# Moving the S5 parameters to GpSimd and the S5 factors to VectorE, and scaling the banded attention's weights without GpSimd

## The chip, the cores and the metric

The kernel runs on one core of a Trainium2 chip. The metric is the device time of one execution in microseconds (us). The core's engines work in parallel, each through its own queue of instructions in a fixed order, and wait for each other on semaphores: TensorE (PE in the profile; PEld is its weight load), VectorE (DVE), ScalarE (ACT), GpSimd (POOL) and SyncE (SP), which starts most of the DMA transfers. A measurement of this kernel tells about 0.3% from no change.

## The reference, cut to what matters

Two residual layers over 1024 tokens of width 1024. Only the first is touched by the change. Its input projection gives q, k, v and a gate for a banded attention with sinks, and u and a gate for an S5 state-space mixer:

```python
def swa_sink_attention(q, k, v, sinks, rel_bias):     # 8 blocks of 128 queries, 8 heads of 64, 2 kv heads
    ...                                               # each block sees its own and the previous 128 keys
    logits = jnp.where(mask[None, :, None, None], logits + bias, NEG_INF)
    p = jax.nn.softmax(jnp.concatenate([logits, sink], axis=-1), axis=-1)[..., :-1]
    out = jnp.einsum('bnhgqk,bnkhd->bnqhgd', p.astype(v.dtype), v_band)

def s5_mixer(u, log_dt, a_re, a_im, b_re, b_im, c_re, c_im, d_skip, glu_w, glu_b):
    dt = jnp.exp(log_dt)[:, None]                     # 32 groups of 64 states
    mag = jnp.exp(a_re * dt)
    ang = a_im * dt
    ab_re, ab_im = mag * jnp.cos(ang), mag * jnp.sin(ang)
    f_re = ((ab_re - 1) * a_re + ab_im * a_im) / (a_re * a_re + a_im * a_im)
    ...
    bb_re = f_re[..., None] * b_re - f_im[..., None] * b_im
    ...                                               # x_t = ab x_(t-1) + bb u_t, y_t = Re(c x_t) + d u_t
    h = jax.nn.gelu(y) @ glu_w + glu_b
    return h[..., :W] * jax.nn.sigmoid(h[..., W:])

def even_layer(hn, ...):
    q, k, v, gate_a, u, gate_b = split_cols(hn @ w_in, EVEN_SPLITS)
    ...                                               # rms norm of q and k by head
    return jnp.concatenate([att * silu(gate_a), ssm * silu(gate_b)], axis=-1) @ w_out
```

The second layer, a sparse attention with an indexer, follows.

## The kernel before

**Weights.** Every projection runs in three TensorE products, high half by high half, high by low and low by high. The weights come as a stream of chunks of 256 columns (8 pieces of 128 x 256): chunk 0 is u's first half, 1 is k and v, 2 is u's second half, 3 and 4 q, 5 and 6 the attention's gate, 7 and 8 the S5 gate, 9 and 10 the GLU, 11 to 18 the first output projection; the second layer's follow. `load_w` (L139) lets ScalarE round a chunk to its high half `whi` (L153) and another engine subtract to the low half `wlo` (L154). That engine is VectorE for the chunks of `LO_ON_V` (L126), in four instructions of 128x512, and otherwise GpSimd, in one of 128x2048 (save for chunks 21, 31 and 32). Such pieces are issued with priority when the stream runs ahead.

**The first 44 us** load x, split it and form u's first half. `mean_square` (L201) then gives 1 / rms of the 1024 tokens: VectorE forms the mean (L209, L210), GpSimd a power of 128x8 (L211), VectorE spreads it on a diagonal (L365), TensorE broadcasts it (L368) and ScalarE copies it to `rb` (L369). All of u's and the gates' results are multiplied by `rb` on VectorE.

**S5 parameters** (L438 to L539) are written next: some 120 VectorE instructions of 128x16, each with a small input from the one ahead. From the state matrix `aa` and the step `dt` they give an exponential (`exp_of`), sine and cosine (ScalarE), the input factors `fre`, `fim`, the powers `pw` of the transition by squaring, the unit rotations `ue` (seven, each squared from the one before and brought back to length one by `unit`), the table `T16` (products of `T` by `ue`, L523 to L528) and `Bb` (L534 to L539).

**Projections of k, v and u** (`u_chunk`, kv) come between. `norm_heads` scales by head: ScalarE squares and sums, GpSimd forms the factor `nr` in two small instructions (L199, L200), ScalarE scales, and for k GpSimd multiplies by the gains (L393).

**S5 quarters.** `s5_quarter` (L589) runs four times. VectorE forms the factors `Q` and `Tb` with `cmul` (L603 to L610 for the code that both engines share); GpSimd forms `W` with the same helper, in 20 instructions per quarter, since its buffer `tmpg` holds 256 elements. TensorE transposes Q into QT and multiplies QT by U (L674). VectorE rotates, scans (L687) and rotates back into X (L690 to L698); TensorE multiplies W by X (L707). While this runs, TensorE works on the remaining projections: the order of every engine's queue was set by a scheduler when the kernel was built, with priorities, so that the k, v, u, q and gate matmuls lie between the quarters' own.

**Banded attention** (215 us and on; after a stretch of gate projection alone, from 252 to 372 us). It runs in 16 units, of a block and a kv head with 4 query heads each. `swa_scores` (L759): TensorE makes scores (L767, L768), VectorE adds the bias and takes the row maximum (L769), ScalarE the exponentials of four heads of 128x256 (L774), VectorE the reciprocal of the sum, and then the weights are scaled: by VectorE in four instructions for kv head 0 (L781), by GpSimd in one of 128x1024 for kv head 1 (L778). `swa_out`: TensorE transposes the weights (L790), ScalarE or VectorE evicts them (L795, L793), and TensorE multiplies by v (L796). Between these lie 384 matmuls of gate projection (L232 to L234) and 36 of the GLU. The GLU, the output projection and the second layer (500 to 1077 us) follow.

## Time and profile before

| | us |
|---|---|
| median of 3 runs | 1075.03 (1072.58 to 1075.17) |
| the profiled execution | 1078.34 |
| its span in the trace | 1076.6 |
| TensorE matmul busy in it | 1012.1 |
| VectorE busy | 770.3 |
| ScalarE busy | 607.1 |
| GpSimd busy | 469.0 |

The granted TensorE clock is 0.983 of full speed on average. The profile gives busy time of each engine, and the views of the trace give each instruction's start and duration and, for idle time, what the engine waited for. A matmul's duration in the trace includes its way through the array: several overlap, so that the time from start to start, not the duration, is what one costs.

### The profile page before, as it was taken

To read this page: it belongs to the slowest core of one execution; us is meant where nothing else is said; L and a number is where in the kernel's file an instruction comes from. 1 tells how busy PE (TensorE), PEld (TensorE's weight loads), DVE (VectorE), ACT (ScalarE), POOL (GpSimd) and SP (SyncE) were. 2 spreads that over 40 slices of the span, in tenths; PEclk is the share of its full clock that TensorE was granted. 3 is DMA by queue.
4 is the path that set the end of the run, shared out by engine and by line. 5 is a ranking of instruction groups with operands and counts; after the bars stand their busy time and mean duration, and the time that the engine had idled before them with its cause. 6 is when DMAs were issued, how large, how long until landed. Compare 5 with 4: busy or idle time off the path is not lost.

```text
span 1076.6 us, 19055 instructions
## 1 busy us (share of the span) xinstructions
PE 1012.1 (94%) x6536; PEld 888.5 (83%) x6536; DVE 770.3 (72%) x1742; ACT 607.1 (56%) x1609; POOL 469.0 (44%) x647
## 2 busy tenths in 40 slices
PE   6898788999999899999999989999999879999998
PEld 4787788999877478887889989999887659898898
DVE  6999889635677675455469678889877997777742
ACT  6453344324545443444466789879976776565620
POOL 2267677332211212223031577867653947555000
PEclk9999899999999899999999999999999999999999
DMA  7282533594343324652011223022325745665333
GB/s 264 79 265 81 149 103 104 151 269 134 96 140 118 103 103 142 210 196 108 1 40 63 67 74 104 16 80 84 98 89 176 246 130 163 200 190 172 115 104 113
DMA packets 103697, 138.33 MB, mean 128 GB/s; under 512 B 9352, under 2 KB 79880, under 8 KB 98736
## 3 DMA queue, kind: packets, MB, share of 16 engines
q1 hardware_dynamic: 103600, 137.12, 39.9%
q8 instruction: 51, 0.84, 0.3%
q14 instruction: 46, 0.38, 0.1%
HBM read 102.31 MB, written 36.21 MB: 129 GB/s over the span
## 4 chain that ended last, share of the span: by engine, by line
PE 68%; DVE 16%; ACT 5%; DMA 4%; POOL 3%; issue 3%; SPq 1%; ACTq 0%; POOLq 0%; DVEq 0%
PE mm L234 7%; PE mm L232 7%; PE mm L233 7%; PE mm L218 4%; PE mm L219 4%; PE mm L220 4%; PE mm L1546 3%; PE mm L1547 3%; PE mm L1545 3%; PE tr L1396 2%; PE psx L796 2%; DVE tmp L687 1%; PE mm L1411 1%; PE mm L1412 1%; PE pq L1370 1%
## 5 line engine op out<-in xcount | busy, mean ns | idle before, releaser
L154 POOL TENSOR_TENSOR wlo<-wraw,whi 128x512 fp32r<-128x512 f32 (+1 forms) x50 | 101.1, 2047 | 111.6 <-ACT whi L153 106.1
L153 ACT CAST whi<-wraw 128x512 fp32r<-128x512 f32 (+2 forms) x122 | 84.3, 748 | 70.6 <-DMA wraw<-in_wo_dram 28.0
L219 PE MATMUL mm<-wlo,h1T_hi 128*128 128x256 f32 x384 | 109.5, 286 | 0.0
L1369 POOL TENSOR_TENSOR bt<-bt,mk 128x384 f32<-128x384 f32 (+3 forms) x80 | 83.8, 1066 | 59.0 <-DMA bt<-g_d 41.0
L218 PE MATMUL mm<-whi,h1T_hi 128*128 128x256 f32 x384 | 109.0, 286 | 0.2 <-DVE gst L976 0.2
L220 PE MATMUL mm<-whi,h1T_lo 128*128 128x256 f32 x384 | 108.9, 285 | 0.0
L1216 DVE TENSOR_SCALAR_CACHE_REDUCE vjunk<-sc,vt 128x512 bf16<-128x512 uint16 (+5 forms) x90 | 91.0, 1012 | 2.7
L233 PE MATMUL mm<-hT_lo,whi 128*128 128x256 f32 (+1 forms) x288 | 86.4, 300 | 0.0
L234 PE MATMUL mm<-hT_hi,wlo 128*128 128x256 f32 (+1 forms) x288 | 86.1, 299 | 0.0
L232 PE MATMUL mm<-hT_hi,whi 128*128 128x256 f32 (+1 forms) x288 | 86.0, 299 | 0.0
L1252 ACT ACTIVATE sjunk<-sc,st 128x384 bf16<-128x384 uint16 (+5 forms) x90 | 77.7, 864 | 6.8 <-POOL st L1256 4.7
L1545 PE MATMUL mm<-aT_hi,whi 128*128 128x256 f32 x256 | 73.0, 285 | 1.2 <-ACT aT_hi L1519 1.2
L218 PEld LDWEIGHTS mm<-whi,h1T_hi 128*128 128x128 f32 x384 | 72.3, 189 | 1.0 <-PE psi L1060 0.6
L1546 PE MATMUL mm<-aT_lo,whi 128*128 128x256 f32 x256 | 72.2, 282 | 0.7 <-DVE aT_lo L1520 0.7
L219 PEld LDWEIGHTS mm<-wlo,h1T_hi 128*128 128x128 f32 x384 | 72.4, 188 | 0.4
L220 PEld LDWEIGHTS mm<-whi,h1T_lo 128*128 128x128 f32 x384 | 72.2, 189 | 0.4
L1547 PE MATMUL mm<-aT_hi,wlo 128*128 128x256 f32 x256 | 72.1, 282 | 0.0
L391 ACT ACTIVATE st<-mm,nr 128x64 f32<-128x64 f32 (+1 forms) x160 | 45.5, 357 | 45.0 <-POOL nr L200 44.6
L154 DVE TENSOR_TENSOR wlo<-wraw,whi 128x512 fp32r<-128x512 f32 (+1 forms) x72 | 50.2, 737 | 25.3 <-ACT whi L153 22.7
L1067 DVE SCALAR_TENSOR_TENSOR sc<-relu,wi,sc 128x384 f32<-128x384 f32 (+3 forms) x70 | 49.4, 707 | 20.6 <-ACT relu L1062 16.9
L1380 ACT ACTIVATE s<-s,mn 128x384 f32<-128x384 f32 (+7 forms) x56 | 45.9, 820 | 26.9 <-DVE mn L1374 26.8
L1400 DVE TENSOR_TENSOR pT_lo<-tr,pT_hi 128x512 fp32r<-128x512 f32 x72 | 49.1, 685 | 15.7 <-ACT pT_hi L1399 15.6
(396 smaller groups left out, 3483.3 us busy)
## 6 DMA issues: line engine op xcount, KB each, us to landing
...
```

What stands on the lines that cost most here:

```text
L153: S.copy(hi[p_], raw[p_])
L154: eng.tensor_sub(lo[p_], raw[p_], rd(hi[p_]))
L218: T.matmul(ps, a, hi[:, k, c0:c1], start=(k == 0), stop=False)
L219: T.matmul(ps, a, lo[:, k, c0:c1], start=False, stop=False)
L220: T.matmul(ps, b, hi[:, k, c0:c1], start=False, stop=(k == 7))
L232: T.matmul(o, a, hT[0][:, k, ts], start=(k == 0), stop=False)
L233: T.matmul(o, a, hT[1][:, k, ts], start=False, stop=False)
L234: T.matmul(o, b, hT[0][:, k, ts], start=False, stop=(k == 7))
L1216: V.tensor_scalar(junk[:, :128 * (b + 1)], data(b), self.thr(j), None, op0=OP.is_ge, op1=OP.add, accum_out=self.cnt[:, it, j:j + 1])
L1545: T.matmul(ps, a, aT[0][:, k, toks], start=(k == 0), stop=False)
L1546: T.matmul(ps, a, aT[1][:, k, toks], start=False, stop=False)
L1547: T.matmul(ps, b, aT[0][:, k, toks], start=False, stop=(k == 7))
```

## The change

Four things change, all in the first layer.

1. **The S5 parameters go to GpSimd.** [...] 34 of them (the exponential of the step, the angle and its reduction) stand ahead of the power for 1 / rms; 115 behind it (the exponential for `mag`, the powers, the squarings and `unit`s of `ue`). An ordering (`issue_after`) holds the sine, the cosine and all that is written up to `Bb` behind the power, the diagonal and rb's copy. The factors `fre`, `fim`, the table `T16` and `Bb` stay on VectorE.
2. **W goes to VectorE**, in 16 instructions per quarter, since the helper's buffer for VectorE holds 512 elements.
3. **Low halves.** Chunks 9 to 12 (the GLU's two and the first two of the output projection) go to VectorE. Those that stay on GpSimd come in four instructions of 128x512.
4. **Scaling of the banded weights.** In every unit two heads are scaled by VectorE and two by ScalarE; GpSimd's instruction goes.

```diff
-    LO_ON_V = (0, 1, 2) + tuple(range(13, 21)) + (29, 30) + tuple(range(33, 39))
+    LO_ON_V = (0, 1, 2) + tuple(range(9, 21)) + (29, 30) + tuple(range(33, 39))
...
-        return (hi, lo), [piece, WSTEP if i in LO_ON_V or i in (21, 31, 32) else 8, 0]
+        return (hi, lo), [piece, WSTEP, 0]
...
-        G.tensor_tensor(r, r, neghalf[:, :n], op=OP.pow)
+        last_rms[0] = G.tensor_tensor(r, r, neghalf[:, :n], op=OP.pow).ins
...
-    def exp_of(sp, o, xin, n):
+    def exp_of(E, stt, sp, o, xin, n):
...
-        V.tensor_scalar(a, xin, 88.0, -87.0, op0=OP.min, op1=OP.max)
+        E.tensor_scalar(a, xin, 88.0, -87.0, op0=OP.min, op1=OP.max)
...
+        def g_stt(o, a, c, b, op0, op1):
+            G.tensor_scalar(stt_t, a, c, None, op0=op0)
+            G.tensor_tensor(o, stt_t, b, op=op1)
+
+        exp_of(G, g_stt, sp, dt, ldt, 16)
...
+        es_late = ExitStack()
+        for i_ in (last_rms[0], dg_mul.ins, rb_copy.ins):
+            es_late.enter_context(tc.issue_after(i_))
+        r2 = q16("r2")
         S.activation(sn, r, AF.Sin)
...
+        exp_of(G, g_stt, sp, mag, tt, 16)
...
         def square(dst, src):
-            V.tensor_mul(small(0), src[:, 0], src[:, 0])
-            V.tensor_mul(small(1), src[:, 1], src[:, 1])
-            V.tensor_sub(dst[:, 0], small(0), small(1))
-            V.scalar_tensor_tensor(dst[:, 1], src[:, 0], 2.0, src[:, 1], op0=OP.mult, op1=OP.mult)
+            G.tensor_mul(sg_[0], src[:, 0], src[:, 0])
+            G.tensor_mul(sg_[1], src[:, 1], src[:, 1])
+            G.tensor_sub(dst[:, 0], sg_[0], sg_[1])
+            g_stt(dst[:, 1], src[:, 0], 2.0, src[:, 1], op0=OP.mult, op1=OP.mult)
...
+            G.tensor_mul(e, e, bc(sg_[0][:, None, :], [128, 2, 16]))
...
+        es_late.close()
...
-        cmul(G, W[:, :, :, 0, :], CT[:, :, js], pw[:, 0, 0, js, None], pw[:, 0, 1, js, None], 16, neg=True)
+        cmul(V, W[:, :, :, 0, :], CT[:, :, js], pw[:, 0, 0, js, None], pw[:, 0, 1, js, None], 16, neg=True)
         for lv, n in enumerate((1, 2, 4)):
-            for a0 in range(0, n, 2):
-                m = min(2, n)
-                cmul(G, Wf[:, :, :, 16 * (n + a0):16 * (n + a0 + m)], Wf[:, :, :, 16 * a0:16 * (a0 + m)],
-                     pw[:, lv, 0, js, None], pw[:, lv, 1, js, None], 16 * m, neg=True)
+            cmul(V, Wf[:, :, :, 16 * n:32 * n], Wf[:, :, :, 0:16 * n], pw[:, lv, 0, js, None], pw[:, lv, 1, js, None],
+                 16 * n, neg=True)
...
-        if kv:
-            G.tensor_mul(s[:, :, :w], s[:, :, :w], bc(den[:, :, None], [128, 4, w]))
-        else:
-            for g in range(4):
+        for g in range(4):
+            if g % 2:
+                S.activation(s[:, g, :w], s[:, g, :w], AF.Copy, scale=den[:, g:g + 1])
+            else:
                 V.tensor_scalar(s[:, g, :w], s[:, g, :w], den[:, g:g + 1], None, op0=OP.mult)
```

The scheduler makes a new order from this. It differs through the banded attention; from the output projection on the same instructions stand in the same order on TensorE but for one of some 3,800. Between the first matmul of the projections behind `rb` and the first W-by-X product of each quarter stand, on TensorE, 234, 378, 518 and 576 projection matmuls of 256 columns before, and 424, 576, 576 and 576 with a further 0, 24, 217 and 417 (gate projection among them; 0, 0, 0 and 77 before) after. Ahead of the first banded score stand 480 gate matmuls before and 671 after; between the banded attention's own stand 384 before and 193 after.

On GpSimd, before, from the power for 1 / rms (L211): the factors for k's heads (`nr`) and the gains follow it.

```order
L211 TENSOR_TENSOR rr<-rr,neghalf 128x8
L199 TENSOR_SCALAR nr<-nms,rr 128x2
L200 TENSOR_TENSOR nr<-nr,neghalf 128x2
L199 TENSOR_SCALAR nr<-nms,rr 128x2
L200 TENSOR_TENSOR nr<-nr,neghalf 128x2
L393 TENSOR_TENSOR st<-st,kg 128x128 x2
```

And after, from the same power (`ex` and `exi` are the exponential's, `stt_t` is the first half of a `g_stt`):

```order
L211 TENSOR_TENSOR rr<-rr,neghalf 128x8
L244 TENSOR_SCALAR ex_443<-tt 128x16
L486 MEMSET CB 128x256
L245 TENSOR_SCALAR ex_444<-ex_443 128x16
L246 TENSOR_SCALAR ex_444<-ex_444 128x16
L443 TENSOR_SCALAR stt_t<-ex_444 128x16
L252 TENSOR_SCALAR exi<-ex_444 128x16
L199 TENSOR_SCALAR nr<-nms,rr 128x2
L444 TENSOR_TENSOR ex_443<-stt_t,ex_443 128x16
L200 TENSOR_TENSOR nr<-nr,neghalf 128x2
L199 TENSOR_SCALAR nr<-nms,rr 128x2
```

The parameters now lie between the factors of k's heads; all 115 of them stand ahead of the first factor of a q tile. Chunk 3's low half (four instructions) lies among them, chunk 4's behind the last, ahead of that factor.

On VectorE, after, from an eviction of u's second half (uT, L566) to the next: the products of `T` by `ue`, which GpSimd now forms, stand between.

```order
L566 TENSOR_TENSOR uT<-mm,rb 128x8x64
L532 TENSOR_TENSOR tm_493<-T_391,ue 128x16
L533 TENSOR_TENSOR tm_494<-T_391,ue 128x16
L534 TENSOR_TENSOR tm_495<-T_391,ue 128x16
L535 TENSOR_TENSOR tm_496<-T_391,ue 128x16
L536 TENSOR_TENSOR T_391<-tm_493,tm_494 128x16
L537 TENSOR_TENSOR T_391<-tm_495,tm_496 128x16
L532 TENSOR_TENSOR tm_493<-T_391,ue 128x32
L533 TENSOR_TENSOR tm_494<-T_391,ue 128x32
L534 TENSOR_TENSOR tm_495<-T_391,ue 128x32
L535 TENSOR_TENSOR tm_496<-T_391,ue 128x32
L566 TENSOR_TENSOR uT<-mm,rb 128x8x64
```

Before, the same products stood ahead of all of u's second half, behind `ue` on VectorE itself (`T` by the last `ue` of four, then `Bb` and the first factor):

```order
L527 TENSOR_TENSOR T_391<-tm_470,tm_471 128x16x8
L528 TENSOR_TENSOR T_391<-tm_472,tm_473 128x16x8
L578 TENSOR_TENSOR kT<-tr,kT 64x512
L534 TENSOR_TENSOR tm_470<-Bt,P_385 128x256
L535 TENSOR_TENSOR tm_471<-Bt,P_385 128x256
```

The uT of u's second half moved up between the products and behind GpSimd's `ue`.

On TensorE, before, near the end of the banded attention: gate projection lies between the transposes (L790), the products with v (L796) and the scores (L767, L768).

```order
L234 MATMUL mm<-hT_hi,wlo 128x256
L232 MATMUL mm<-hT_hi,whi 128x256
L233 MATMUL mm<-hT_lo,whi 128x256
L790 MATMUL tr<-ident,s 128x128
L234 MATMUL mm<-hT_hi,wlo 128x256
L790 MATMUL tr<-ident,s 128x128
L232 MATMUL mm<-hT_hi,whi 128x256
L790 MATMUL tr<-ident,s 128x128
L233 MATMUL mm<-hT_lo,whi 128x256
```

After, in its second half (the lines are 5 further down):

```order
L795 MATMUL tr<-ident,s 128x128 x8
L772 MATMUL psx<-kT,qT 128x256
L773 MATMUL psx<-kT,qT 128x256
L772 MATMUL psx<-kT,qT 128x256
L773 MATMUL psx<-kT,qT 128x256
L801 MATMUL psx<-pT,vt 64x512 x2
L772 MATMUL psx<-kT,qT 128x256
L773 MATMUL psx<-kT,qT 128x256
```

No other work lies between the attention's own there: the gate projection has run out at the eighth of the 16 units, and the GLU's 36 matmuls at the ninth.

## Rows read from the trace of the kernel before

**Rows 1.** The page's first part: busy time, share of the span and instructions of each engine.

```profile
PE 1012.1 (94%) x6536; PEld 888.5 (83%) x6536; DVE 770.3 (72%) x1742; ACT 607.1 (56%) x1609; POOL 469.0 (44%) x647
```

**Rows 2.** Busy time by stretches of the span. Columns: length of the stretch, busy time and instructions of PE (matmul), PEld (weight load), DVE (VectorE), ACT (ScalarE) and POOL (GpSimd), the granted TensorE clock, the DMA share and GB/s.

```profile
43.70:97.00 53.30, 47.99 (x311) 40.47 (x311) 49.27 (x149) 24.10 (x108) 33.82 (x50) 0.97 0.61 190
97.00:130.00 33.00, 23.16 (x183) 22.12 (x182) 28.99 (x52) 11.78 (x46) 21.98 (x27) 0.84 0.40 118
130.00:150.00 20.00, 16.84 (x118) 16.07 (x118) 19.19 (x38) 7.54 (x49) 19.24 (x28) 0.91 0.20 57
150.00:215.00 65.00, 59.71 (x497) 57.55 (x497) 53.64 (x97) 29.47 (x137) 34.57 (x38) 0.95 0.47 136
...
252.00:300.00 48.00, 46.75 (x351) 41.24 (x351) 34.21 (x126) 24.30 (x77) 14.01 (x5) 1.00 0.39 122
...
343.00:372.00 29.00, 26.22 (x95) 14.16 (x95) 21.26 (x41) 17.32 (x34) 8.76 (x3) 0.88 0.35 127
```

**Rows 3.** What the matmul side of TensorE waited for between 0 and 330 us: total us, times, longest us.

```profile
PE ps L707 <- DVE X L698: 11.7, 3, 7.6
...
PE tr L368 <- DVE sq L365: 3.6, 1, 3.6
```

**Rows 4.** GpSimd's and then VectorE's instructions in order of time near 110 us: start, duration, engine, line, operation, out<-in with shapes and count.

```profile
108.36 4.94 POOL L154 TENSOR_TENSOR wlo<-wraw,whi 128x2048 fp32r<-128x2048 f32 x1
...
108.87 4.58 DVE L603 TENSOR_TENSOR tmp<-Q,pw 128x128 f32<-128x128 f32 x1
113.48 1.69 DVE L698 TENSOR_TENSOR X<-tmp 64x512 f32<-64x512 f32 x2
```

**Rows 5.** Busy time by stretches of 2 us, columns as in rows 2.

```profile
110.00:112.00 2.00, 0.00 (x0) 0.00 (x0) 2.00 (x1) 0.00 (x0) 2.00 (x1) 1.00 0.02 4
...
116.00:118.00 2.00, 2.00 (x11) 2.00 (x10) 1.90 (x7) 0.00 (x0) 1.11 (x2) 0.50 0.74 311
```

**Rows 6.** GpSimd's instructions grouped by line and shape: the costliest and the cheapest of the ten groups of the W factors and, between them, the factors of k's heads (30 to 215 us), and low halves of 512 elements (whole span). Columns: count, busy us, mean ns, idle before them.

```profile
L604 POOL TENSOR_TENSOR tmpg<-W,pw 128x256 f32<-128x256 f32 x12 | 9.4, 782 | 0.0
...
L200 POOL TENSOR_TENSOR nr<-nr,neghalf 128x2 f32<-128x2 f32 x8 | 5.9, 740 | 0.6
L199 POOL TENSOR_SCALAR nr<-nms,rr 128x2 f32<-128x2 f32 x8 | 5.1, 638 | 10.9 <-ACT st L388 10.9
...
L603 POOL TENSOR_TENSOR tmpg<-W,pw 128x128 f32<-128x128 f32 x4 | 1.6, 405 | 0.2
...
L154 POOL TENSOR_TENSOR wlo<-wraw,whi 128x512 fp32r<-128x512 f32 x40 | 54.0, 1382 | 34.0 <-ACT whi L153 34.0
```

**Rows 7.** VectorE's instructions in order of time: four back-to-back products and sums of the S5 factors.

```profile
182.78 0.28 DVE L609 TENSOR_TENSOR Q<-tmp 128x128 f32<-128x128 f32 x1
182.98 0.28 DVE L610 TENSOR_TENSOR Q<-tmp 128x128 f32<-128x128 f32 x1
183.30 0.69 DVE L603 TENSOR_TENSOR tmp<-Q,pw 128x512 f32<-128x512 f32 x1
183.91 0.68 DVE L604 TENSOR_TENSOR tmp<-Q,pw 128x512 f32<-128x512 f32 x1
```

**Rows 8.** TensorE's instructions in order of time, cut: three of the first of 256 columns behind the broadcast of 1 / rms.

```profile
50.16 0.87 PE L218 MATMUL mm<-whi,hT_hi 128*128 128x256 f32 x1
...
50.98 0.28 PE L220 MATMUL mm<-whi,hT_lo 128*128 128x256 f32 x1
51.10 0.29 PE L218 MATMUL mm<-whi,hT_hi 128*128 128x256 f32 x1
```

**Rows 9.** GpSimd's instructions in order of time, cut to the power for 1 / rms and two short ones that follow each other for one tile's head factors.

```profile
43.53 1.71 POOL L211 TENSOR_TENSOR rr<-rr,neghalf 128x8 f32<-128x8 f32 x1 [24.86 <-DVE rr L210]
...
58.88 0.29 POOL L199 TENSOR_SCALAR nr<-nms,rr 128x2 f32<-128x2 f32 x1
59.26 0.71 POOL L200 TENSOR_TENSOR nr<-nr,neghalf 128x2 f32<-128x2 f32 x1
```

**Rows 10.** Instructions grouped by line and shape, columns as in rows 6: GpSimd's scaling of the banded weights, ScalarE's exponentials (same shape as the new scalings), and VectorE's three groups that an attention unit always needs.

```profile
L778 POOL TENSOR_TENSOR s<-s,den 128x1024 f32<-128x1024 f32 x7 | 13.3, 1895 | 66.6 <-DVE den L776 40.0 <-ACT mm L421 12.4 <-PE psx L796 8.8
...
L774 ACT ACTIVATE s<-s,nm 128x256 f32<-128x256 f32 x56 | 27.8, 497 | 33.1 <-DVE nm L770 33.1
...
L769 DVE CUSTOM_DVE_ANT_0 s<-psx,bm 128x256 f32<-128x256 f32 x56 | 22.8, 418 | 9.7 <-PE psx L768 9.5
L781 DVE TENSOR_SCALAR s<-s,den 128x256 f32<-128x256 f32 x28 | 12.3, 498 | 0.2
L793 DVE COPY pT<-tr 128x512 f32<-128x512 f32 x14 | 9.6, 682 | 5.3 <-PE tr L790 4.0 <-PE psx L796 1.3
```

**Rows 11.** GpSimd's, VectorE's and TensorE's instructions in order of time at the end of the banded attention.

```profile
352.88 4.97 POOL L154 TENSOR_TENSOR wlo<-wraw,whi 128x2048 fp32r<-128x2048 f32 x1 [6.33 <-ACT whi L153]
...
353.39 4.48 DVE L771 TENSOR_TENSOR sd<-snk,nm 128x4 f32<-128x4 f32 x1
...
359.97 1.03 PE L790 MATMUL tr<-ident,s 128*128 128x128 f32 x4 [1.49 <-DVE s L781]
362.01 1.97 PE L796 MATMUL psx<-pT,vt 128*64 128x512 f32 x2 [1.01 <-DVE pT L793]
```

**Rows 12.** GpSimd's and VectorE's instructions in order of time near 14 us.

```profile
13.66 5.01 POOL L343 TENSOR_TENSOR acc<-acc,sq 128x1024 f32<-128x1024 f32 x2 [9.82 <-ACT sq L341]
...
13.86 2.36 DVE L459 TENSOR_TENSOR den<-aa 128x16 f32<-128x16 f32 x1
```

More of the change, by code (lines that the diff above doesn't have):

```diff
@@ L368, in tile_hybrid_swa_s5_dsa @@
             T.matmul(pt, ones, dg[:, 4 * half:4 * half + 4].rearrange("p i t -> p (i t)"), start=True, stop=True)
-            S.copy(rb[:, half * 512:(half + 1) * 512], pt)
+            rb_copy = S.copy(rb[:, half * 512:(half + 1) * 512], pt)
     with tc.tile_pool(name="bias0", bufs=1, reuse_waits="tile") as bp:
@@ L438, in tile_hybrid_swa_s5_dsa @@
         dt = q16("dt")
[L439 removed]
+        stt_t = q16("stt_t")
+        def g_stt(o, a, c, b, op0, op1):
+            G.tensor_scalar(stt_t, a, c, None, op0=op0)
+            G.tensor_tensor(o, stt_t, b, op=op1)
+        exp_of(G, g_stt, sp, dt, ldt, 16)
         tt, ang, k, r = q16("tt"), q16("ang"), q16("k"), q16("r")
         mag, cs, sn, fre, fim = (P5[:, i, :] for i in range(5))
[L442 to L446 removed]
+        G.tensor_mul(tt, are, dt)
+        G.tensor_mul(ang, aim, dt)
+        G.tensor_scalar(k, ang, 1.0 / (2 * math.pi), MAGIC, op0=OP.mult, op1=OP.add)
+        G.tensor_scalar(k, k, MAGIC, None, op0=OP.subtract)
         c1 = 6.28125
@@ L484, in tile_hybrid_swa_s5_dsa, with unit @@
         tm = [sp.tile([128, 256], F32, name=f"tm{i}") for i in range(4)]
-        def small(i):
-            return tm[i][:, :16]
         mg, c_, s_ = P5[:, 0], P5[:, 1], P5[:, 2]
-        V.tensor_mul(pw[:, 0, 0], mg, c_)
-        V.tensor_mul(pw[:, 0, 1], mg, s_)
+        sg_ = [q16(f"sg{i}") for i in range(2)]
+        G.tensor_mul(pw[:, 0, 0], mg, c_)
+        G.tensor_mul(pw[:, 0, 1], mg, s_)
         def square(dst, src):
-            V.tensor_mul(small(0), src[:, 0], src[:, 0])
-            V.tensor_mul(small(1), src[:, 1], src[:, 1])
-            V.tensor_sub(dst[:, 0], small(0), small(1))
-            V.scalar_tensor_tensor(dst[:, 1], src[:, 0], 2.0, src[:, 1], op0=OP.mult, op1=OP.mult)
+            G.tensor_mul(sg_[0], src[:, 0], src[:, 0])
+            G.tensor_mul(sg_[1], src[:, 1], src[:, 1])
+            G.tensor_sub(dst[:, 0], sg_[0], sg_[1])
+            g_stt(dst[:, 1], src[:, 0], 2.0, src[:, 1], op0=OP.mult, op1=OP.mult)
         square(pw[:, 1], pw[:, 0])
         square(pw[:, 2], pw[:, 1])
+        def unit(e):
+            G.tensor_mul(sg_[0], e[:, 0], e[:, 0])
+            G.tensor_mul(sg_[1], e[:, 1], e[:, 1])
+            G.tensor_add(sg_[0], sg_[0], sg_[1])
+            G.tensor_scalar(sg_[0], sg_[0], -0.5, 1.5, op0=OP.mult, op1=OP.add)
+            G.tensor_mul(e, e, bc(sg_[0][:, None, :], [128, 2, 16]))
         square(ue[:, 0], P5[:, 1:3])
@@ L503, in tile_hybrid_swa_s5_dsa @@
         square(ue[:, 0], ue[:, 1])
-        def unit(e):
-            V.tensor_mul(small(0), e[:, 0], e[:, 0])
-            V.tensor_mul(small(1), e[:, 1], e[:, 1])
-            V.tensor_add(small(0), small(0), small(1))
-            V.tensor_scalar(small(0), small(0), -0.5, 1.5, op0=OP.mult, op1=OP.add)
-            V.tensor_mul(e, e, bc(small(0)[:, None, :], [128, 2, 16]))
         unit(ue[:, 0])
@@ L593, in tmp @@
             return s5q.tile([128, 512], F32, name="tmp", bufs=4)
-        def tmpg():
-            return s5q.tile([128, 256], F32, name="tmpg", bufs=2)
         def cmul(eng, o, a, b_re, b_im, n, neg=False):
             b2 = [128, 2, 4, n]
-            t, u = ((tmpg if eng is G else tmp)()[:, :8 * n].rearrange("p (t j n) -> p t j n", t=2, j=4)
+            t, u = (tmp()[:, :8 * n].rearrange("p (t j n) -> p t j n", t=2, j=4)
                     for _ in range(2))
```

41 lines of the change are left out of this document (18 added, 23 removed).

## The prediction

> **What bounds the kernel now.** I read the page's busy times first: TensorE's matmuls fill 94% of the span, the next engine 72% [rows 1]. So a gain can come only from the stretches in which TensorE idles or runs below full clock. The view by stretches finds them [rows 2]. Between 43.7 and 215 us, where the S5 branch runs among projections, TensorE idles 53.30 - 47.99 = 5.3, 9.8, 3.2 and 5.3 us: 23.6. The granted clock there is 0.97, 0.84, 0.91 and 0.95; the share missing is 1.6 + 5.3 + 1.8 + 3.3 = 12 us of these stretches, of which I count three quarters, 9 us, as work that was slowed (the rest fell on idle time). Together 32.6 us are lost. Around the banded attention 1.25 + 2.8 us idle and 0.12 x 29 x 3/4 = 2.6 us of clock are lost: 6.6. The instructions behind it keep their order, and I take nothing from them. The wait view names the largest loss: the product of W and X (L707) waited 11.7 us in three waits for VectorE's X, the longest 7.6; the broadcast of 1 / rms waited 3.6 [rows 3]. The timeline says why X was late: GpSimd's low half of 128x2048 started at 108.36 and took 4.94 us, and a VectorE multiply of 128x128 that began at 108.87 ended with it, 4.58 us long; X was written only behind it, until 115.2 [rows 4]. The multiply itself is a small one. TensorE stood wholly still at 110 to 112, and at 116 to 118 its clock was 0.50, the lower level, behind that idle time [rows 5]. So the long wait comes from what GpSimd holds up on VectorE, not from VectorE's own amount of work.
>
> **The change in the S5 stage.** *What goes.* 117 small instructions leave VectorE, which had ended the parameters at about 64 us, well ahead of X; that by itself moves no end. W's instructions leave GpSimd, 9.4 us in the costliest of ten groups [rows 6]. On VectorE a quarter's W is 8 products and 8 sums; from start to start 128 elements take 0.20 us and 512 take 0.61 [rows 7], 0.34 and 0.13 by proportion for 256 and 64: 2 x (0.20 + 0.20 + 0.34 + 0.61) + 2 x (0.13 + 0.13 + 0.20 + 0.34) = 4.3 us a quarter. A quarter has 20 us or more, so most of that is covered by waits of VectorE for matmuls; if it falls into the chain to X it costs its full 4.3. I take 1.5 us for what is left of each X wait, 6 in all: no 5 us block remains, but pieces of 512 (1.38 us mean [rows 6]) do, and W stands ahead of X in the queue.
>
> *1 / rms.* Twelve more projection matmuls stand ahead of the broadcast on TensorE, at 0.12 us each [rows 8]: the wait falls from 3.6 to about 2.
>
> *The chain on GpSimd.* The power for 1 / rms ends at 43.53 + 1.71 = 45.2 [rows 9]. 115 small instructions follow. No instruction of 128x16 on GpSimd stands in the trace. The nearest are the pair for one tile's head factors: 0.29 us for the first, 0.38 from its start to the start of the dependent one [rows 9]. I take 0.33, the middle, 38 us, with 33 and 44 as ends. Between them stand k's eight pairs (8 us at 0.29 + 0.71, 11 at the groups' 0.64 + 0.74; I take 9), eight gains at 0.41 by the 128x128 row, 3.3, and the four pieces of chunk 3's low half, 4 x 1.38 = 5.5 [rows 6, 9]. So **the last unit rotation `ue` lands at 45.2 + 38 + 9 + 3.3 + 5.5 = 101 us**. Behind it come chunk 4's four pieces, 5.5, and with M's clearing and the first q tile's factor, of four heads, some 3 more: 109.5. Behind this chain queue, on VectorE, the T16 products, and behind those the evictions of u's second half; on ScalarE, the scalings of q, and behind them on TensorE q's transposes.
>
> *What TensorE has meanwhile.* From 50.2 [rows 8]: 144 matmuls of k and v at 0.12 = 17; 96 of 512 columns, twice that, 22.5; 69 of q, three tiles, at which its PSUM buffers hold tiles that ScalarE can't scale yet, 8.2; transposes of k 1: near 99. u's second half waits now and then for VectorE, which stands behind `ue`: I take 2.5 us, about two of the four evictions late by a little over 1 us. Transposes of Q then carry it to about 104, and **some 6 us are idle until the first q tile's factor at 109.5**. Later the queue is better filled than before: 340 more projection matmuls (41 us) stand ahead of the fourth quarter's X, moved up from later stretches, so that the X waits of the last three quarters have cover. Other evictions cost 2, the clock after idle times 4.
>
> Sum for the stage: 2 + 2.5 + 6 + 6 + 2 + 4 = 22.5 against 32.6, a gain of **10.1 us**.
>
> **The change in the banded attention.** GpSimd's seven scalings of 1.9 us go [rows 10]. The block at the end goes too: a VectorE sum of four numbers took 4.48 us, begun 0.5 us into a GpSimd low half of 4.97 [rows 11]. On ScalarE 32 scalings of 128x256 arrive; the exponential of that shape takes 0.497 [rows 10], a plain scaling no more, and at two a unit it adds at most 1 us. But 191 of the gate matmuls that moved up (23 us) come out of this stretch. Before, gate projection lay between all of the units; now it ends at the eighth and the GLU's at the ninth. In the last units, then, TensorE has its own eight transposes (2.1 us), two products with v (about 1, since the 1.97 were at half clock) and eight scores (0.95): 4 us [rows 8, 11]. VectorE has 4 x 0.418 + 2 x 0.498 + 0.682 = 3.35 and some 0.6 of small ones: 4 [rows 10]. With both at 4 and each handing to the other, I take 0.5 us of TensorE idle time a unit over eight units, 4 for the drain at the end (1.49 + 1.01 us of waits stood in two rows before [rows 11]) and 2 for the clock: 10 against 6.6, **3.4 us given back**. Low halves of four more chunks on VectorE (0.6 us an instruction) lie in the same stretch; VectorE has room for these in the first units.
>
> **A page on this.** The block at 108.87 also bears out a rule: the Trainium skill, page "SBUF — State Buffer", section "Who interferes with whom", says that VectorE and GpSimd share a pair of ports as an exclusive lock, held for a whole instruction by whoever came first, and that a VectorE instruction with two SBUF inputs contends with GpSimd's reads. The trace agrees: 4.58 us for a multiply, where sums of its size take 0.28 [rows 7]. By it the 115 small GpSimd instructions would each hold up VectorE's by at most their own 0.33; if that fell on every second one, 19 us of VectorE's time would go, most of it while VectorE waits for `ue` anyway, and the sum would stand.
>
> **The rivals.**
> *The chain is slower.* If a small instruction takes 0.38 from start to start, `ue` lands 6 us later, TensorE idles 12 instead of 6, and each quarter's X comes 1.5 later: +12, 1080. It decides when the last `ue` lands after some 105 us. For it: k's pairs took 1.38 together in the mean, above the 1.0 of the best pair [rows 6, 9]. Against it: T16 needs only the first four rotations, and q matmuls are there to move up.
> *The attention without cover gives all back.* If in eight units VectorE and TensorE alternate rather than overlap, they lose 1.2 us more apiece: 10 in all, 1075, no change.
> *The waits vanish.* If the X waits and the drain are hidden by the moved projections, 6 + 4 go as well: 1058, and 1055 with part of what the chain's short end, 33 us, saves. For it: only one of the three X waits was long, and its cause is removed.
> *The lock ahead of 1 / rms.* 34 GpSimd instructions now run beside VectorE's rounding of x. Before, a 16-element VectorE sum took 2.36 us beside GpSimd's sums of 5.01 [rows 12]. 34 x 0.33 = 11 us of overlap, less some 3 of small VectorE work that leaves and 4 of slack in the load: +4.5, 1073. The rule on the shared pair, of the same page and section, speaks for this one; on VectorE's instructions from PSUM it would not bear.
>
> **How the numbers follow.** The profiled execution took 1078.34 for a span of 1076.6, 3.3 above the median of 1075.03; I carry the difference of the sum, 10.1 - 3.4 = 6.7, over to the median: **1068.3, say 1068**. Chances: this forecast 0.45; the slow chain 0.20; attention without cover 0.11; waits vanish 0.17; the lock 0.07. What can be told from no change is 0.3%, 3.2 us. Faster by more: the forecast but for 0.02 of it, the vanishing waits and 0.02 of the lock, 0.43 + 0.17 + 0.02 = 0.62. Within: the uncovered attention, 0.02 of the forecast and 0.05 of the lock, 0.18. Slower: the slow chain, 0.20. The range opens at 1055, the vanishing waits', and closes at 1081, just above the slow chain's; what is left out is the far side of these two, some two in ten. The forecast's own range, by the ends 33 and 44 us of the chain, is 1063 to 1074.
>
> **What would show it.** GpSimd's last `ue` instruction near 101; TensorE's idle time between 97 and 112 near 6 us; X waits of at most 2 us each; no VectorE instruction of over 2 us beside a low half; in the last units of the attention TensorE idle about half a us a unit, and the clock at 1.00 save for its end. I am wrong in the chain if `ue` lands beyond 105, in the cover if TensorE's idle time in the attention exceeds 12 us, and in the load if the power for 1 / rms starts later than 45.

## The result and the profile after

The changed kernel takes 1066.26 us (median of 5 runs, 1061.45 to 1070.71) against 1075.17 (1072.58 to 1078.13): a ratio of 0.9912, with a 95% interval of 0.9888 to 0.9935, so 7 to 12 us faster. The forecast was 1068, faster. The profiled execution took 1065.89 us for a span of 1064.2.

The page's first part, to be read beside [rows 1]:

```profile
PE 1013.1 (95%) x6536; PEld 890.5 (84%) x6536; DVE 748.7 (70%) x1705; ACT 622.3 (58%) x1671; POOL 436.5 (41%) x722
```

VectorE and GpSimd are some 20 and 30 us less busy and ScalarE 15 us more. TensorE has the same number of matmuls. The view by the same stretches as [rows 2], with the one of 300 to 343 us added:

```profile
43.70:97.00 53.30, 50.74 (x318) 45.55 (x317) 27.79 (x74) 25.40 (x115) 48.45 (x150) 0.97 0.61 189
97.00:130.00 33.00, 30.68 (x260) 29.21 (x258) 29.61 (x69) 19.02 (x100) 18.25 (x17) 0.95 0.38 109
130.00:150.00 20.00, 18.48 (x175) 17.42 (x175) 16.39 (x50) 11.74 (x63) 7.83 (x12) 1.00 0.64 185
150.00:215.00 65.00, 62.12 (x517) 60.31 (x516) 63.94 (x145) 20.73 (x70) 17.53 (x16) 0.97 0.46 129
...
252.00:300.00 48.00, 46.55 (x346) 40.45 (x344) 31.29 (x129) 31.96 (x96) 2.00 (x2) 1.00 0.68 178
300.00:343.00 43.00, 40.42 (x187) 24.31 (x186) 35.59 (x136) 34.50 (x107) 0.00 (x0) 1.00 0.44 127
343.00:372.00 29.00, 25.61 (x101) 15.88 (x100) 16.56 (x28) 14.41 (x32) 0.00 (x0) 1.00 0.31 92
```

Between 43.7 and 215 us TensorE now idles 2.6 + 2.3 + 1.5 + 2.9 = 9.3 us, where it was 23.6 before, and the granted clock is 0.95 or more in each of these stretches. From 300 to 372 us it idles 2.6 + 3.4 us, but these two rows are not those of before over again: the banded attention ends at 352.8 us here, and at 371.0 there. In the fourth row VectorE is busy 63.94 of 65 us: S5 quarters now leave it no pause. TensorE's waits, total, times and longest (compare [rows 3]):

```profile
PE ps L651 <- DVE Q L616: 5.1, 3, 2.1
PE mm L218 <- ACT st L392: 2.6, 1, 2.6
...
PE tr L369 <- DVE sq L365: 1.8, 1, 1.8
...
PE ps L712 <- DVE X L703: 1.6, 3, 0.9
```

The three X waits are 1.6 us together (11.7 before), and that for 1 / rms is 1.8 (3.6). New is a wait for the factor Q of 5.1 us in three. GpSimd in order of time:

```profile
39.59 1.68 POOL L211 TENSOR_TENSOR rr<-rr,neghalf 128x8 f32<-128x8 f32 x1
...
51.14 0.22 POOL L444 TENSOR_TENSOR ex<-stt_t,ex 128x16 f32<-128x16 f32 x1
51.45 0.25 POOL L443 TENSOR_SCALAR stt_t<-ex 128x16 f32<-128x16 f32 x1
...
55.36 0.21 POOL L504 TENSOR_TENSOR sg<-pw 128x16 f32<-128x16 f32 x1
55.55 0.27 POOL L443 TENSOR_SCALAR stt_t<-pw 128x16 f32<-128x16 f32 x1
...
81.52 0.25 POOL L517 TENSOR_TENSOR ue<-ue,sg 128x32 f32<-128x32 f32 x1
...
89.53 0.25 POOL L517 TENSOR_TENSOR ue<-ue,sg 128x32 f32<-128x32 f32 x1
...
95.88 1.14 POOL L199 TENSOR_SCALAR nr<-nms,rr 128x4 f32<-128x4 f32 x2
```

The power for 1 / rms starts at 39.59 us, 3.9 earlier than before [rows 9]. Behind it stand the small instructions, 0.3 us from start to start where one needs the other (51.14 to 51.45), and 0.2 where it doesn't (55.36 to 55.55). The fourth unit rotation ends at 81.8 us, the last at 89.8, the first q factor comes at 95.88.

**The sections of the span.** The view by line gives the first and last start of each line. From it come these marks of the two profiled executions, in us:

| | before | after |
|---|---|---|
| power for 1 / rms starts | 43.5 | 39.6 |
| first, last product of W and X | 114.4, 214.4 | 126.9, 236.1 |
| first banded score | 251.2 | 255.8 |
| last product of banded weights and v | 371.0 | 352.8 |
| last power for 1 / rms, of the second layer | 509.5 | 492.4 |
| end of the span | 1076.6 | 1064.2 |

The marks lie over different amounts of work, since gate projection has moved. (Of the 480 and 671 matmuls that the section on the change counts ahead of the first score, 96 are of u's second half; the gates' own are 384 and 575.) At 0.119 us each, from start to start (0.12 in [rows 8]), the 191 are 22.7 us. Taken off, the first score comes at 255.8 - 22.7 = 233.1, 18.1 us earlier than before; given back to the attention, this lasts 97.0 + 22.7 = 119.7, against 119.8. So in this pair the whole gain lies ahead of the first score. From the attention's end to that last power the profile after is 1.1 us longer, and from there to the end 4.7 longer, where both kernels issue the same.

### The profile page after: what moved, and what is told of

It is laid out like the page before. It is cut to its first block, busy times and chain, and to the rows that moved or that the text cites. A ratio compares the mean times of both kernels' runs of the same rounds, so it can differ in the third digit from the quotient of the medians.

```text
span 1064.2 us, 19143 instructions
## 1 busy us (share of the span) xinstructions
PE 1013.1 (95%) x6536; PEld 890.5 (84%) x6536; DVE 748.7 (70%) x1705; ACT 622.3 (58%) x1671; POOL 436.5 (41%) x722
## 3 DMA queue, kind: packets, MB, share of 16 engines
q1 hardware_dynamic: 103600, 137.12, 41.3%
## 4 chain that ended last, share of the span: by engine, by line
PE 68%; DVE 14%; POOL 6%; ACT 5%; DMA 3%; issue 3%; SPq 1%; ACTq 0%; POOLq 0%; DVEq 0%
PE mm L234 8%; PE mm L232 8%; PE mm L233 8%; PE mm L218 5%; PE mm L219 5%; PE mm L220 5%; PE mm L1551 3%; PE mm L1552 3%; PE mm L1550 3%; PE psx L801 2%; PE tr L1401 2%; PE mm L1416 1%; PE mm L1417 1%; PE pq L1375 1%; PE tr L795 1%
## 5 line engine op out<-in xcount | busy, mean ns | idle before, releaser
L153 ACT CAST whi<-wraw 128x512 fp32r<-128x512 f32 (+1 forms) x152 | 87.3, 643 | 74.4 <-PE mm L233 38.2
L154 POOL TENSOR_TENSOR wlo<-wraw,whi 128x512 fp32r<-128x512 f32 x64 | 87.3, 1391 | 96.3 <-ACT whi L153 96.3
L919 POOL TENSOR_TENSOR acc<-acc,sq 128x512 f32<-128x512 f32 x12 | 18.1, 1507 | 195.4 <-DVE wlo L154 154.0
L154 DVE TENSOR_TENSOR wlo<-wraw,whi 128x512 fp32r<-128x512 f32 (+1 forms) x88 | 62.9, 760 | 15.1 <-ACT whi L153 12.7
```

The lines of the kernel that those rows point to most:

```text
L153: S.copy(hi[p_], raw[p_])
L154: eng.tensor_sub(lo[p_], raw[p_], rd(hi[p_]))
```

## The experiments

Twelve kernels ran beside the kernel before. A part is one of the four of the section on the change. Every edit makes the scheduler lay a new order, so that each run shows a part together with the order that goes with it. For each, two marks of its profiled execution stand here beside the time: the first banded score, corrected to 384 gate matmuls ahead of it, and the attention's length, corrected to 384 within it, both at 0.119 us.

| run | parts | median, us | ratio to before (95%) | first score | attention |
|---|---|---|---|---|---|
| before | none | 1075.0 to 1076.8 | 1 | 251.2 | 119.8 |
| e1_lo_alone | 3 | 1075.17 | 0.9993 (0.9978 to 1.0008) | 242.1 | 116.1 |
| e2_params_alone | 1 | 1077.9 | 1.001 (0.9988 to 1.0032) | 247.4 | 119.4 |
| e3_w_alone | 2 | 1072.1 | 0.996 (0.994 to 0.9981) | 242.1 | 118.3 |
| e4_scale_alone | 4 | 1077.84 | 1.0017 (0.9998 to 1.0036) | 247.1 | 118.8 |
| e11_w_lo | 2, 3 | 1064.68 | 0.9889 (0.9868 to 0.9909) | 237.8 | 114.4 |
| e6_no_params | 2, 3, 4 | 1061.49 | 0.9862 (0.9836 to 0.9887) | 239.8 | 110.2 |
| e7_no_w | 1, 3, 4 | 1066.47 | 0.9912 (0.9892 to 0.9933) | 243.2 | 111.5 |
| e5_no_lo | 1, 2, 4 | 1065.47 | 0.9904 (0.9882 to 0.9925) | 236.2 | 122.3 |
| e8_no_scale | 1, 2, 3 | 1066.42 | 0.9909 (0.988 to 0.9938) | 232.5 | 118.4 |
| changed | all | 1066.26 | 0.9912 (0.9888 to 0.9935) | 233.1 | 119.7 |
| e10_early_only | 34 instructions of 1; 2, 3, 4 | 1061.95 | 0.9866 (0.9844 to 0.9887) | 235.7 | 114.8 |
| e9_hold_gate | all, gate held | 1081.17 | 1.0043 (1.0025 to 1.006) | 253.2 | 117.8 |
| e12_hold_both | all, gates held | 1072.59 | 0.9971 (0.9953 to 0.9988) | 249.5 | 111.4 |

Executions of one kernel differ by several us, and each profile is one of them. That of e1_lo_alone is the shortest of its 13 (1066.52 against a median of 1075.17), so that its marks flatter it. That of e8_no_scale is the shortest of its 6 (1062.29), that of e5_no_lo the longest of its 8 (1070.96). The first score of before, 251.2, is late beside that of e4_scale_alone, whose edit doesn't touch what lies ahead (247.1). Differences of 5 us and more between marks are read here, or those that several runs repeat.

### One part alone

e1_lo_alone, part 3:

```diff
-    LO_ON_V = (0, 1, 2) + tuple(range(13, 21)) + (29, 30) + tuple(range(33, 39))
+    LO_ON_V = (0, 1, 2) + tuple(range(9, 21)) + (29, 30) + tuple(range(33, 39))
...
-        return (hi, lo), [piece, WSTEP if i in LO_ON_V or i in (21, 31, 32) else 8, 0]
+        return (hi, lo), [piece, WSTEP, 0]
```

> The kernel before with part 3 of the change alone: GpSimd's low halves in instructions of 128x512, chunks 9 to 12 on VectorE. Theory A (the gain in the S5 stage comes from the end of the 4.6 us blocks that a 128x2048 low half puts on VectorE, and that of the first 44 us from the parameters leaving VectorE): the 7.6 us wait for X shrinks to 2 or less, 4 to 7 us faster than before, and 1 / rms stays at 43.5 us. Rival B (GpSimd's amount of work, W above all, makes X late): X still comes late, 0 to 2 us faster.

e2_params_alone, part 1 (the excerpt of its diff in the section on the change, from `last_rms` to `es_late.close()`):

```diff
-        exp_of(sp, dt, ldt, 16)
+        exp_of(G, g_stt, sp, dt, ldt, 16)
```

> The kernel before with part 1 alone: the S5 parameters on GpSimd, W and the low halves as before. Theory A: the power for 1 / rms starts 3.5 to 4 us earlier (near 39.6 us), but the low halves of 128x2048 and W now stand behind 115 small instructions on GpSimd, so that part or all of it is lost in the S5 stage: 0 to 4 us faster. Rival C (the parameters' move is the change's whole gain): 8 to 10 us faster.

With it VectorE's instructions fall from 1742 to 1625 and GpSimd's rise from 647 to 796: 117 have become 149.

e3_w_alone, part 2:

```diff
-        cmul(G, W[:, :, :, 0, :], CT[:, :, js], pw[:, 0, 0, js, None], pw[:, 0, 1, js, None], 16, neg=True)
+        cmul(V, W[:, :, :, 0, :], CT[:, :, js], pw[:, 0, 0, js, None], pw[:, 0, 1, js, None], 16, neg=True)
```

> The kernel before with part 2 alone: W on VectorE. Theory A: VectorE's 4.3 us a quarter fall into its waits, and the long wait for X, which a low half makes, stays: within 2 us of before. Rival B: X waits go, 4 to 8 us faster.

e4_scale_alone, part 4:

```diff
-        if kv:
-            G.tensor_mul(s[:, :, :w], s[:, :, :w], bc(den[:, :, None], [128, 4, w]))
-        else:
-            for g in range(4):
+        for g in range(4):
+            if g % 2:
+                S.activation(s[:, g, :w], s[:, g, :w], AF.Copy, scale=den[:, g:g + 1])
+            else:
```

> The kernel before with part 4 alone: the banded weights scaled by VectorE and ScalarE. Theory A: with gate projection between all units the scaling lies in TensorE's shadow: within 2 us of before. Rival D (GpSimd's 1.9 us scalings delay the transposes and hold up VectorE): 3 to 5 us faster.

Only W alone gains, 4.3 us by its ratio. Neither theory came whole. Theory A's main claim falls in its first form: part 3 does end the long X wait, but its median gains nothing that can be told. The gain of W alone is rival B's in size, but not in its reason, since most of the X waits stayed, 7.9 of 11.7 us:

```profile
PE ps L702 <- DVE X L693: 7.9, 3, 3.6
```

TensorE's waits in e1_lo_alone:

```profile
PE tr L404 <- ACT st L391: 3.9, 4, 1.9
...
PE ps L707 <- DVE X L698: 3.4, 2, 1.7
```

X waits went from 11.7 to 3.4 us; 3.9 us of q's transposes waiting for ScalarE's scaling stayed (4.1 before). That wait belongs to W on GpSimd: a q tile's factor queues there between W's instructions. It grows where the parameters stand in the same queue, in e2_params_alone

```profile
PE tr L405 <- ACT st L392: 9.5, 1, 9.5
```

and in e7_no_w, the changed kernel with W back on GpSimd:

```profile
PE tr L405 <- ACT st L392: 10.3, 3, 6.1
```

None of the kernels with W on VectorE has it among its larger waits but e10_early_only, with 1.0 us. The attention holds a second block, which part 2 alone leaves. GpSimd and VectorE near the end of it in e3_w_alone, and then TensorE's wait:

```profile
341.25 6.42 POOL L154 TENSOR_TENSOR wlo<-wraw,whi 128x2048 fp32r<-128x2048 f32 x1 [22.03 <-ACT whi L153]
348.26 1.92 POOL L773 TENSOR_TENSOR s<-s,den 128x1024 f32<-128x1024 f32 x1 [0.59 <-DVE nm L765]
```

```profile
343.16 4.52 DVE L770 TENSOR_TENSOR den<-den,sd 128x4 f32<-128x4 f32 x1
```

```profile
PE tr L785 <- POOL s L773: 5.9, 1, 5.9
```

A low half of 128x2048 runs from 341.25 for 6.42 us, VectorE's sum of four numbers takes 4.52 beside it, GpSimd's scaling stands behind it until 348.26, and TensorE's transposes wait 5.9 us for that scaling. This is the block that [rows 11] showed in the kernel before, with the scaling's queue added.

### One part undone

Each is the changed kernel with one part as in the kernel before. e5_no_lo:

```diff
-        return (hi, lo), [piece, WSTEP, 0]
+        return (hi, lo), [piece, WSTEP if i in LO_ON_V or i in (21, 31, 32) else 8, 0]
```

> The changed kernel with part 3 undone: GpSimd's low halves of 128x2048 again, chunks 9 to 12 on GpSimd. Theory E (the parts help each other: the parameters' chain on GpSimd pays only when W and the long low halves are off that engine): 3 to 5 us slower than the changed kernel, near 1070. Rival F (the parts add up as they measured alone, -0.8, +1, -4.3 and +1.8): within 1 us of the changed kernel, 1067.

e6_no_params:

```diff
-        exp_of(G, g_stt, sp, dt, ldt, 16)
+        exp_of(sp, dt, ldt, 16)
```

> The changed kernel with part 1 undone: the S5 parameters on VectorE, all else changed. Theory E: 1 / rms comes at 43.5 us again and the gain falls to W's and a little, 1070 to 1073. Rival F: 1065, since the parameters alone cost 1 us.

e7_no_w:

```diff
-        cmul(V, W[:, :, :, 0, :], CT[:, :, js], pw[:, 0, 0, js, None], pw[:, 0, 1, js, None], 16, neg=True)
+        cmul(G, W[:, :, :, 0, :], CT[:, :, js], pw[:, 0, 0, js, None], pw[:, 0, 1, js, None], 16, neg=True)
```

> The changed kernel with part 2 undone: W on GpSimd, behind the parameters' chain there. Theory E: W's products come late for every quarter; most of the gain goes, 1074 to 1078. Rival F: 4.3 us slower, 1070.6.

e8_no_scale:

```diff
+        if kv:
+            G.tensor_mul(s[:, :, :w], s[:, :, :w], bc(den[:, :, None], [128, 4, w]))
```

> The changed kernel with part 4 undone: the banded weights of kv head 1 scaled by GpSimd again. Theory G (with the gate projection run out, GpSimd's 1.9 us lie on the path of the last seven units): 2 to 5 us slower than the changed kernel. Rival F: 1.8 us faster, 1064.5.

None came as Theory E had it. Of Rival F's four, e5_no_lo came as it said, e8_no_scale can't be told from it (1066.4 for 1064.5), and e6_no_params and e7_no_w came some 4 us faster. Undoing part 2, 3 or 4 changes the changed kernel's time by nothing that can be told, and undoing part 1 makes it 4.8 us **faster** (the intervals of the two ratios just don't overlap, 0.9888 and up against 0.9887 and down). Theory G falls too, for e8_no_scale. The four parts alone add up to some -2 us against -8.9 for all of them. What holds the kernel with part 1 is shown by its stages beside those of e6_no_params: from the power for 1 / rms to the first product of W and X, to the last one, to the first score, and to the end of the attention. The changed kernel:

```profile
39.60:126.90 87.30, 80.88 (x570) 73.74 (x569) 58.01 (x148) 45.01 (x219) 67.39 (x168) 0.96 0.51 156
126.90:236.10 109.20, 104.58 (x884) 101.19 (x883) 100.47 (x224) 39.17 (x151) 34.36 (x33) 0.98 0.44 124
236.10:255.80 19.70, 19.00 (x161) 18.81 (x160) 4.32 (x7) 3.03 (x6) 3.91 (x2) 1.00 1.04 287
255.80:352.80 97.00, 92.82 (x537) 65.17 (x537) 69.78 (x271) 71.24 (x215) 0.00 (x0) 1.00 0.49 139
```

And e6_no_params:

```profile
44.70:111.60 66.90, 58.43 (x385) 49.99 (x383) 63.81 (x186) 31.73 (x139) 31.69 (x39) 0.97 0.57 169
111.60:221.00 109.40, 104.35 (x869) 101.29 (x870) 96.91 (x222) 46.92 (x219) 42.25 (x40) 0.95 0.45 128
221.00:240.40 19.40, 19.40 (x164) 19.40 (x164) 4.76 (x8) 2.96 (x6) 3.91 (x2) 1.00 1.03 287
240.40:349.90 109.50, 108.04 (x724) 85.52 (x723) 78.11 (x279) 76.44 (x224) 5.04 (x4) 1.00 0.47 140
```

The three quarters between the first and the last product take the same 109 us in both, with VectorE busy for 100.5 and 96.9 of them. But the first product comes at 126.9 us with part 1 and at 111.6 without, 15.3 later, although 1 / rms came 5.1 earlier. VectorE's first instruction for the quarter's factor Q starts at 90.33 us in the changed kernel, behind the T16 products that waited for GpSimd's `ue`, and at 72.03 in e6_no_params:

```profile
90.33 1.73 DVE L622 COPY Q<-Bb 128x128 f32<-128x128 f32 x1
```

```profile
72.03 0.23 DVE L612 COPY Q<-Bb 128x128 f32<-128x128 f32 x1
```

TensorE fills the time with gate projection (570 matmuls up to the first product, for 385) that would otherwise lie in the attention, which then runs with 537 matmuls in place of 724 in 97.0 us, where 109.5 - 187 x 0.119 = 87.2 would be its share. So the gate projection that went ahead is missed in the attention by 9.8 us. Ahead of it part 1 gains 6.7, as the corrected first score comes at 233.1 instead of 239.8; the difference, 3 us in this pair of profiles, is most of the 4.8 by which the medians differ.

e11_w_lo has parts 2 and 3, by the two diffs above.

> The kernel before with parts 2 and 3 together: W on VectorE and the low halves in instructions of 128x512. Theory L (the two together make nearly the whole gain, since a low half of 128x2048 holds up VectorE in the S5 stage and again near the end of the banded attention, where the scaling on GpSimd stands behind it): 10 to 14 us faster than before, as the run without the parameters' move. Rival M (the scaling's part is needed as well): 5 to 8 us faster.

It is 12 us faster than before: Theory L. Alone the two parts had come to some 5 together, so that the rest is what each does only with the other. With part 4 (e6_no_params) the median falls by 3.2 us more, and the attention's corrected length from 114.4 to 110.2. The intervals of the two ratios overlap, so a part of the scaling where the attention is covered is likely and not shown. In the changed kernel, whose attention isn't covered, undoing it changes nothing.

e10_early_only moves the 34 instructions ahead of the power alone:

```diff
-        exp_of(G, g_stt, sp, mag, tt, 16)
+        exp_of(V, V.scalar_tensor_tensor, sp, mag, tt, 16)
...
-        G.tensor_mul(pw[:, 0, 0], mg, c_)
+        V.tensor_mul(pw[:, 0, 0], mg, c_)
...
-            G.tensor_mul(sg_[0], src[:, 0], src[:, 0])
+            V.tensor_mul(sg_[0], src[:, 0], src[:, 0])
```

> The changed kernel with only the 34 parameter instructions ahead of the power for 1 / rms on GpSimd; the 115 behind it on VectorE, as in the kernel before. Theory J (the parameters' move gains in the first 44 us, by small instructions that leave VectorE there, and loses behind them): 1 / rms near 40 us, the rest as in the run without the parameters' move, so 3 to 5 us faster than that run, near 1057. Rival K (VectorE's later start on the remaining parameters makes the first quarter late again): 1061 to 1064.

Rival K: 1061.95, as e6_no_params. 1 / rms came at 40.5 us, 4.2 earlier, but the first product of W and X at 117.7, 6.1 later, as VectorE began the remaining parameters only behind 1 / rms, at 44.0 us, where e6_no_params has the same instruction at 37.1.

### The gate projection held back

e9_hold_gate keeps the S5 gate's matmuls behind the first score, which in the changed kernel went ahead of it by 191:

```diff
+    first_score, gate_n = [None], [0]
...
+              gate_n[0] += 1
+              with behind([first_score[0]] if gate_n[0] > 8 else []):
...
+            sc_ = T.matmul(o, qT[:, h, :], kT[:, kv, k0:k0 + w], start=True, stop=False)
+            first_score[0] = first_score[0] or sc_.ins
```

> The changed kernel with the S5 gate's 384 projection matmuls held behind the first banded score on TensorE, so that none of them lies in the S5 stage (191 do in the changed kernel). Theory H (the cover that was moved up is missing in the banded attention and costs 8 to 10 us there): the banded attention, corrected for its matmuls, is 8 to 10 us shorter, and the kernel 5 to 9 us faster than the changed one, near 1058 to 1061. Rival I (these matmuls covered waits in the S5 stage, which come back without them): the banded attention gains and the S5 stage loses the same, 1064 to 1068.

It is 0.4% slower than before, by a wait that neither theory named. The queue of SyncE, and then TensorE's wait:

```profile
236.60 0.33 SPq L719 DMA_DIRECT2D y_d<-Y  x1
...
238.72 1.64 SPq L746 DMA_DIRECT2D snk<-in_sinks_dram  x1
240.40 3.80 SPq L750 DMA_DIRECT2D bm<-g_d  x6
...
247.14 2.66 SPq L762 DMA_DIRECT2D qT<-qT_d  x4
```

```profile
PE psx L776 <- DMA qT<-qT_d: 17.3, 1, 17.3
```

The S5 stage's last store is issued at 236.6; then come the sinks and the bias tiles, and q's loads only at 247.14. TensorE had nothing left for 17.3 us. Nor is the attention 8 to 10 us shorter, as Theory H had it, but 117.8 for 119.7. Its first stretch, behind the idle time, ran at a granted clock of 0.85, so that this run alone doesn't decide on the cover:

```profile
253.20:275.00 21.80, 21.79 (x161) 21.80 (x162) 11.70 (x60) 9.85 (x37) 1.95 (x1) 0.85 0.60 119
```

In the changed kernel gate projection fills the 17 us without q (161 matmuls between 236.1 and 255.8 in its rows above). e12_hold_both leaves 144 of the attention gate's matmuls for them:

```diff
+              with behind([first_score[0]] if gate_n[0] > 8 else [last_x[0]] if gate_n[0] > 5 else []):
...
+                last_x[0] = xm_.ins
```

> The changed kernel with the S5 gate's matmuls held behind the first banded score, and the last 144 of the attention gate's held behind the last product of W and X, so that work is left for the 17 us in which the first queries are loaded. Theory H (the cover that was moved up is missing in the banded attention, and the S5 stage does not need it): the first banded score near 235 us instead of 256, the attention about 110 us long for some 730 matmuls of 256 columns (97 for 537 in the changed kernel), the kernel 5 to 9 us faster than the changed one, 1057 to 1061. Rival I (the S5 stage needs these matmuls as cover): the last product of W and X comes later than 225 us, and the kernel stays at 1064 to 1068.

Its stages from the first product of W and X on:

```profile
125.20:232.30 107.10, 87.36 (x707) 83.45 (x706) 95.18 (x218) 35.54 (x148) 29.20 (x29) 0.89 0.43 123
232.30:249.50 17.20, 17.20 (x148) 17.20 (x147) 2.84 (x5) 1.81 (x3) 3.90 (x2) 1.00 0.94 258
249.50:360.90 111.40, 109.92 (x729) 86.38 (x728) 78.57 (x279) 76.95 (x224) 5.02 (x4) 1.00 0.45 136
```

The attention does what Theory H said: 111.4 us for 729 matmuls. But the three quarters took 107.1 us with 177 matmuls fewer, and TensorE idled 19.7 of these at a granted clock of 0.89: the kernel is 6.3 us slower than the changed one. That is Rival I's sign (its last product was to come past 225 us, and came at 232.3), with a higher price than it gave. The quarters' length hardly depends on TensorE's work, then, and what TensorE is given there is nearly free; the same work is worth some 8 us in the attention. There isn't enough of it for both.

## Why the prediction came out as it did

The forecast, 1068, holds the time. Its direction is right, the long X wait and the block in the attention ended as it said, and its price of a small GpSimd instruction was near. That the sum is within 2 us is in part luck. In this pair of profiles the S5 stage gained 18.1 us for 10.1, the attention lost nothing for 3.4, and 5.8 were lost behind it, where the sum had nothing.

- **What bounds the kernel.** The long X wait came from a 128x2048 low half: it shrank to 3.4 us in e1_lo_alone with that edit alone. But on the time it was worth little by itself (e1_lo_alone, 0.9993). W, which the prediction priced only for VectorE, holds up q's factors on GpSimd; its move alone was worth 4.3.
- **W on VectorE.** "Most of that is covered" fell: VectorE is busy 63.94 of 65 us between 150 and 215, and the three quarters take 109 us with W there in the changed kernel, where they took 100 before. Over all profiles they take 107 to 112 us in the nine kernels with W on VectorE, and 94 to 105 in the five with W on GpSimd. The term of 1.5 us for each X wait was too high all the same, as the waits are 1.6 us together; but Q's waits, 5.1 us, had no term, and the 6 in all come out near by that.
- **The first 44 us.** No gain was in the sum, and the rival of the lock put a loss of 4.5 there. Measured: 1 / rms starts 3.9 us earlier. VectorE before, cut to a small instruction, the last sum of squares and the mean:

```profile
16.34 2.35 DVE L245 TENSOR_SCALAR ex<-ex 128x16 f32<-128x16 f32 x1
...
36.28 1.23 DVE L343 TENSOR_TENSOR acc<-acc,sq 128x1024 f32<-128x1024 f32 x1
...
42.95 0.17 DVE L209 TENSOR_SCALAR rr<-tr 128x8 f32<-128x8 f32 x1 [0.89 <-PE tr L208]
```

  and after, the last two sums of squares and the mean:

```profile
30.27 1.23 DVE L343 TENSOR_TENSOR acc<-acc,sq 128x1024 f32<-128x1024 f32 x1
...
32.70 1.24 DVE L343 TENSOR_TENSOR acc<-acc,sq 128x1024 f32<-128x1024 f32 x1
38.41 0.17 DVE L209 TENSOR_SCALAR rr<-tr 128x8 f32<-128x8 f32 x1 [4.48 <-PE tr L208]
```

  Two small instructions of 2.36 [rows 12] and 2.35 us, held up beside GpSimd's sums (the 5.01 us in [rows 12] are two sums, and VectorE's is a product), are gone, and the last sum of squares comes at 32.70 instead of 36.28. It is GpSimd that now waits. (The page of the Trainium skill that the prediction names, "SBUF — State Buffer", section "Who interferes with whom", gives the shared ports to whoever issues first; these rows agree, and the prediction looked at one side of it.) Its small instructions, first beside VectorE's instructions of 128x1024 and then after these have ended:

```profile
30.52 1.12 POOL L443 TENSOR_SCALAR stt_t<-ex 128x16 f32<-128x16 f32 x1
31.72 1.14 POOL L444 TENSOR_TENSOR ex<-stt_t,ex 128x16 f32<-128x16 f32 x1
...
35.09 0.25 POOL L443 TENSOR_SCALAR stt_t<-ex 128x16 f32<-128x16 f32 x1
35.43 0.22 POOL L444 TENSOR_TENSOR ex<-stt_t,ex 128x16 f32<-128x16 f32 x1
...
39.44 0.20 POOL L459 TENSOR_SCALAR r<-r 128x16 f32<-128x16 f32 x1
```

  1.12 us against 0.25 to 0.3. The chain of 34 ends at 39.64, and the power starts 0.8 us behind VectorE's mean (38.78) for it.
- **The chain on GpSimd.** It was to end at 101 us and ended at 89.8: it began 4 us earlier, and a small instruction costs some 0.27 us in the mean, not 0.33, and so 7 us less in all. (From 41.3 to 89.8 are 48.5 us; without k's pairs, gains and low halves, some 17 us, 31 are left for 115, 0.27 each.) The slow chain, the one rival on the other side, lands nowhere near.
- **TensorE's idle time behind it.** Predicted 6 us between 97 and 112; measured 2.1. They are one wait for Q (2.1 us); the first q factor, for which they were to be, came at 95.88. The reading of the chain stopped too early: that GpSimd ends sooner than feared doesn't make the first quarter start sooner than before. Its factor Q stands on VectorE behind the T16 products and two evictions of u, and the first product of W and X comes 12.5 us later than before and 15.3 later than without part 1 (e6_no_params). The prediction saw this queue, took 2.5 us for u's evictions in it and let Q's transposes follow near 104; what its sum has no term for is that all quarters then begin later than before.
- **The S5 stage as a whole.** 10.1 us of gain were predicted, 18.1 measured in this pair of profiles, of which some 4 is the late first score of the one of before (251.2, against 247.1 in e4_scale_alone).
- **The attention.** 3.4 us of net loss were predicted, 0 measured. The mechanism is the predicted one, and both halves were too small. For the cover that moved away the sum has half a us a unit over eight units and 2 for the clock, 6 in all. By the marks it costs 8 to 10 (119.7 against 111.4 in e12_hold_both and 110.2 in e6_no_params), near the 10 of the rival without cover. The end of GpSimd's blocks with the scaling gains about as much (119.8 before, against 110.2 and, in e7_no_w, 111.5 where the cover is left). The sign that the prediction named, TensorE's idle time, doesn't show the cost: it is 97.0 - 92.8 = 4.2 us, since a matmul with none behind it counts as busy for its whole duration, 0.28 us where one in a stream costs 0.12 [rows 8].
- **What the change is worth in its parts.** Parts 2 to 4 make 13.7 us, and part 1 costs 4.8 of these; the prediction, too, had only costs for it behind 1 / rms, but not this one. The fastest kernels here are e6_no_params and e10_early_only, 1061.5 and 1062.0, faster than both.

What stays open: why the time after the last 1 / rms differs between profiles (below). That the chain on GpSimd, made shorter, would bring the first quarter forward was not tried.
